# Hybrid decoder block on one core: the Strassen combinations of h (T1 to T4) made on GpSimd instead of VectorE

## Chip, cores and metric

The kernel runs on one NeuronCore of a Trainium2 chip. The metric is the device time of one execution in microseconds; lower is better. The engines are called TensorE (PE in the views; PEld is its weight load), VectorE (DVE), ScalarE (ACT), GpSimd (POOL) and SyncE (SP, which issues nearly all DMAs here).

## The reference

One decoder block with S = 2048 rows, D = 1024 features, fp32 in and out. Cut to what matters:

```python
mod = c @ W_ada + b_ada                         # shift, scale, gate for mixer and FFN
h = rms_norm(x, g_pre) * (1 + scale) + shift
p = h @ W_in                                    # one combined input projection
# split into attention q|k|v, mLSTM q|k|v|o, mLSTM i|f pre-gates, branch gates A|B
yA = sliding_window_attention(rope(q), rope(k), v, sinks)     # window 128, 8 q heads, 2 kv heads
yB = sigmoid(o) * norm(mlstm_chunkwise(silu(conv4(q)), silu(conv4(k)), v, i, f))
merged = sigmoid(gA) * (yA @ W_A) + sigmoid(gB) * (yB @ W_B)
x = x + gate * rms_norm(merged @ W_out)
x = x + gate2 * rms_norm(swiglu(modulate(rms_norm(x))))       # FFN with its own W's
```

What concerns the change is `h` and a part of `h @ W_in`.

## The kernel before

**fp32 by halves.** TensorE multiplies in a reduced fp32 form (`fp32r`). Each operand is split into a high part (a cast) and a low part (the residue), and a product is three matmuls: hi by hi, hi by lo, lo by hi. For weights `split` makes them: ScalarE casts `whi` (L259, L256 where heads are paired), VectorE subtracts for `wlo` (L260, L257). For h, ScalarE writes the cast (L518) and the full value (L520) from the transposed block in PSUM, and VectorE writes the residue (L521); in the first block GpSimd does L521.

**Blocks.** The rows go in four blocks of 512 (`TB`), numbered 0 to 3, and two blocks make a superblock. `hprep(b)` makes h of block b, transposed, feature tile by feature tile (`one(k)`, eight of them). The wide columns of W_in are multiplied for a superblock at a time by a Strassen-Winograd scheme with seven products; h is its 2 x 2 grid: feature half by row block. The scheme needs, besides h itself, four combinations T1 to T4, each a 128 x 4 x 512 tile. The even block leaves two of the full-precision h tiles in T1 and T4, the odd block two in T3 and T2; after each pair of feature tiles `one(k)`, `one(k + 4)` of an odd block four subtractions in place (L534 to L537) finish column k of all four:

```python
T1 = T3 - T1;  T3 = T2 - T3;  T2 = T2 - T1;  T4 = T4 - T2
```

That is 16 subtractions of 128 x 512 in block 1 and 16 in block 3, 32 in all. `hsums` later copies a finished T tile by DMA (L545, issued by SP) into the buffer of its low part, casts it (L551, ScalarE) and subtracts (L552, VectorE): first for T2 and T4, later for T1 and T3. `pair_parts` then uses them in the seven products.

**What runs around it.** While blocks 1 and 3 are prepared, TensorE multiplies the k, v, q, o and gate columns of the even block with plain three-matmul products (accumulators `acc`, weights `whi` and `wlo`); VectorE also makes rotary embeddings of q and k (L757 to L761, with L771/L772 and L797/L798 for the transposed copies), the moving convolution of gate columns (L810 to L813), and softplus and scans of the gates (L835 to L868, with the transposes mix_1070 and mix_1120 on TensorE). ScalarE moves accumulators out of PSUM (L827 and others). Then follows attention for the even block: loads by SP (L903 to L908), scores, mask (L933), maximum (L938), exponential (L946, ScalarE), normalisation (L950, GpSimd), transposes (L956, issued through L209), and the products with v. L428 is the accumulation of `c W_ada`.

**What sets the order.** The Python code writes these stages as generators (streams) that yield estimated delays; `tick` and `finish` interleave them by a running estimate of TensorE's time. The framework's compile-time scheduler (`schedule_with_timeline_sim=True`) then orders each engine's instructions again by its own model. On the chip each engine runs its list in order and waits at semaphores. `mm` and `transpose` all issue through one line each, L204 and L209, so TensorE's rows are told apart by tile.

Of the kernel before, what the change touches and what calls it, by code (L numbers as in the profile page):

```python
# [15 lines left out]
ALU = mybir.AluOpType  # L16
# [55 lines left out]
def decoder_block(ctx: ExitStack, tc: tile.TileContext, a: dict, out: bass.AP, dbg=None):  # L72
    nc = tc.nc
    V, A, G, T = nc.vector, nc.scalar, nc.gpsimd, nc.tensor
# [18 lines left out]
    def nm(s):  # L93
        uid[0] += 1
        return f"{s}{uid[0]}"
# [4 lines left out]
    def mix_tile():  # L100
        return ps_mix.tile([P, 512], F32, tag="mix", name=nm("mix"))
# [7 lines left out]
    def big(shape, dtype=F32):  # L109
        t = bpool.tile([P, 2048], dtype, tag="big", name=nm("big"))  # L110
        return t.rearrange("p (k c) -> p k c", k=shape[0])
# [4 lines left out]
    def load_x(src, big, i):  # L116
        xb = big([2, D])
        nc.sync.dma_start(xb, src[i * 256:(i + 1) * 256, :].rearrange("(t p) c -> p t c", p=P))
        return xb
# [86 lines left out]
    def transpose(o, i):  # L206
        now[0] += 110.0
        k = i.shape[0]
        T.transpose(o, i, ident[:k, :k])  # L209
# [260 lines left out]
    def rsqrt_of_sumsq(ss, n, eps=EPS):  # L470

        ms = small.tile([P, 4], F32, tag="ms", name=nm("ms"), bufs=4)
        V.tensor_scalar(ms[:, :n], ss, 1.0 / D, eps, op0=ALU.mult, op1=ALU.add)  # L473
        r = small.tile([P, 4], F32, tag="rs", name=nm("rs"), bufs=6)
        G.tensor_tensor(r[:, :n], ms[:, :n], nhalf[:, :n], op=ALU.pow)  # L475
        return r
# [3 lines left out]
    def hc_part(name, i):  # L480
        st = HC.setdefault(name, [None, None])
        if st[i] is None:
            st[i] = big([4, TB], F32R)
        return st[i]

    def hprep(b, first=False):

        odd = b % 2
        xs = []
        xbs = x_first if first else [load_x(x_d[b * TB:(b + 1) * TB, :], big, i) for i in range(2)]  # L490
        V_NAMES = ("T3", "T2") if odd else ("T1", "T4")
        for n in V_NAMES:
            HR[n] = big([4, TB])
        vs = [HR[n] for n in V_NAMES]
        for i in range(2):
            xb = xbs[i]
            ss = small.tile([P, 4], F32, tag="ss", name=nm("ss"), bufs=4)
            for t in range(2):
                for hf in range(2):
                    A.activation(vs[i][:, 2 * t + hf, :], xb[:, t, hf * 512:(hf + 1) * 512], AF.Square,  # L500
                                 accum_out=ss[:, 2 * hf + t:2 * hf + t + 1])
            V.tensor_tensor(ss[:, 0:2], ss[:, 0:2], ss[:, 2:4], op=ALU.add)
            r = rsqrt_of_sumsq(ss[:, 0:2], 2)
            for t in range(2):
                if first:
                    A.activation(xb[:, t, :], xb[:, t, :], AF.Copy, scale=r[:, t:t + 1])
                else:
                    V.tensor_scalar(xb[:, t, :], xb[:, t, :], r[:, t:t + 1], None, op0=ALU.mult)
                xs.append(xb[:, t, :])
        yield L_X  # L510

        def one(k):
            name = f"{k // 4 + 1}{odd + 1}"
            hi, lo = (hc_part(name, i)[:, k % 4, :] for i in range(2))
            ps = mix_tile()
            for t in range(NT):
                transpose(ps[:, t * P:(t + 1) * P], xs[t][:, k * P:(k + 1) * P])
            A.activation(hi, ps, AF.Identity, scale=s1[:, k:k + 1], bias=sh1[:, k:k + 1])  # L518
            v = vs[k // 4][:, k % 4, :]
            A.activation(v, ps, AF.Identity, scale=s1[:, k:k + 1], bias=sh1[:, k:k + 1])  # L520
            (G if first else V).tensor_tensor(lo, v, hi.bitcast(F32), op=ALU.subtract)  # L521

        if not odd:
            for k in range(KD):
                one(k)
                yield L_HT
            return
        for k in range(4):
            one(k)
            yield L_HT  # L530
            one(k + 4)
            yield L_HT
            t1, t2, t3, t4 = (HR[n][:, k, :] for n in ("T1", "T2", "T3", "T4"))
            V.tensor_tensor(t1, t3, t1, op=ALU.subtract)  # L534
            V.tensor_tensor(t3, t2, t3, op=ALU.subtract)
            V.tensor_tensor(t2, t2, t1, op=ALU.subtract)
            V.tensor_tensor(t4, t4, t2, op=ALU.subtract)  # L537
            yield L_HT

    def hsums(names):  # L540
# [170 lines left out]
    def c_tile(n):  # L711
        C[n] = kvp.tile([P, MH, MD + 1], F32, tag="cst", name=nm("cst"), bufs=3)
        return C[n]

    hp0 = hprep(0, first=True)
    next(hp0)
    tables = {}
# [18 lines left out]
    def superblock(sb):  # L736
# [474 lines left out]
        def outputs(b):  # L1211
# [41 lines left out]
            def before_out():  # L1253
                if b == 0:
                    finish(R["ada_m"])
                    R_ada.append(spawn(ada_stream([(4, "scale"), (3, "shift"), (5, "gate")], 9000.0)))
                if b == b1 and b + 1 < NBLK:
                    HC.clear()
                    hps[b + 1] = spawn(hprep(b + 1))
                    tables[sb + 1] = rope_tables(sb + 1)  # L1260
                R["gg"] = big([2, D])[:, 0, :]
                nc.sync.dma_start(R["gg"], gg_m_d)
                if b == b0:
                    end_attention(2 * NT)
                    load_y(b1, 0)
                    load_g(b1, 0)
# [11 lines left out]
        def start():  # L1278
            hps[b1] = spawn(hprep(b1), L_HP2)
# [590 lines left out]
```

## Time and profile before

| | |
|---|---|
| median of 3 runs | 2711.97 us (2708.91 to 2712.32) |
| profiled execution, its own time | 2716.59 us |
| span of the profiled execution | 2714.9 us |
| mean granted TensorE clock | 0.99 |
| busy TensorE / VectorE / ScalarE / GpSimd | 2639.2 / 1986.2 / 1299.8 / 148.2 us |
| DMA | 511.90 MB, mean 189 GB/s |

A row of a timeline has start and duration in microseconds, then engine, line, operation, output tile, input tiles, shapes and types, a count, and in brackets the idle time before it with what ended that. Instructions of one engine overlap at their ends, so the price of one in a row of equal ones is the distance of their starts, not the duration. Tiles are named without numbers in the views of the trace and with them in the order of instructions.

### The profile page before, as it was taken

The numbers are of one execution on the slowest core, as the hardware profiler recorded it, in microseconds if no ns is written. First come the engines' busy times: TensorE is split into PE (matmuls) and PEld (weight loads), VectorE is DVE, ScalarE is ACT, GpSimd is POOL, SyncE is SP. The second block draws the span as 40 slices with busy tenths as digits, with TensorE's granted clock in tenths as the row PEclk, the third lists the DMA queues.
The fourth block names the chain that finished last, engine by engine and source line by source line (L and its number), as shares of the span: only waits on it lengthen the run. The fifth ranks groups of instructions, "written<-read, shape, count | busy, mean of one in ns | idle before, by whom it ended". The sixth has DMA issues, their size and how long they took to land.

```text
span 2714.9 us, 35793 instructions
## 1 busy us (share of the span) xinstructions
PE 2639.2 (97%) x12310; PEld 2138.9 (79%) x12310; DVE 1986.2 (73%) x3906; ACT 1299.8 (48%) x2558; POOL 148.2 (5%) x189
## 2 busy tenths in 40 slices
PE   6989999999998999999999999999999999999998
PEld 4867788888885678888887888888877888888886
DVE  7968788778695778876687777776677676766456
ACT  5556544444755564444563443335554333333444
POOL 2010001100101000110000000000000000000000
PEclk8999999999998999999999999999999999999999
DMA  7654355897574544678765564436675232324566
GB/s 249 206 184 157 128 172 179 269 340 248 196 235 147 196 138 138 213 231 291 251 224 198 175 201 152 155 113 213 215 271 188 97 117 86 113 97 144 186 210 217
DMA packets 353639, 511.90 MB, mean 189 GB/s; under 512 B 25120, under 2 KB 213660, under 8 KB 348208
## 3 DMA queue, kind: packets, MB, share of 16 engines
q1 hardware_dynamic: 353456, 509.61, 56.9%
q8 instruction: 97, 1.59, 0.2%
q14 instruction: 86, 0.70, 0.1%
HBM read 357.12 MB, written 144.02 MB: 185 GB/s over the span
## 4 chain that ended last, share of the span: by engine, by line
PE 85%; DVE 7%; DMA 4%; ACT 2%; issue 1%; POOL 0%; SPq 0%; DVEq 0%; ACTq 0%; POOLq 0%
PE acc L204 61%; PE mix L204 22%; PE mix L209 2%; DVE hl L1357 1%; DVE tm L428 1%; DMA raw<-as_d 1%; ACT tm L946 1%; ACT hl L1356 1%; DMA raw<-in_w_in_dram 1%; DMA at_d<-tx 0%; DMA big<-in_x_dram 0%; DVE wlo L260 0%; DMA tx<-in_w_ada_dram 0%; DVE w L1667 0%; DMA at<-at_d 0%
## 5 line engine op out<-in xcount | busy, mean ns | idle before, releaser
L204 PE MATMUL acc<-big,hl 128*128 128x512 f32 x3936 | 940.8, 394 | 4.3 <-ACT tx L827 1.8
L204 PEld LDWEIGHTS acc<-big,hl 128*128 128x128 f32 x3936 | 733.3, 188 | 172.5 <-issue 13.8
L1356 ACT CAST hl<-raw 128x512 fp32r<-128x512 f32 x732 | 440.1, 621 | 493.4 <-PE acc L204 222.2
L1357 DVE TENSOR_TENSOR hl<-raw,hl 128x512 fp32r<-128x512 f32 x732 | 496.3, 694 | 194.8 <-ACT hl L1356 194.0
L204 PE MATMUL acc<-whi,big 128*128 128x512 f32 (+1 forms) x1280 | 379.3, 377 | 10.8 <-ACT big L518 8.4
L204 PEld LDWEIGHTS acc<-whi,big 128*128 128x128 f32 x1280 | 236.2, 192 | 52.4 <-ACT big L518 8.5
L204 PE MATMUL mix<-big,hl 128*128 128x512 f32 x1056 | 263.9, 391 | 1.7 <-ACT hl L1356 1.1
L204 PE MATMUL acc<-wlo,big 128*128 128x512 f32 (+1 forms) x640 | 241.2, 379 | 6.4 <-DVE wlo L260 6.4
L204 PE MATMUL acc<-hl,hl 128*128 128x512 f32 x1008 | 237.4, 393 | 5.1 <-DVE hl L1357 3.4
L204 PEld LDWEIGHTS mix<-big,hl 128*128 128x128 f32 x1056 | 197.9, 188 | 45.9 <-ACT hl L1356 1.9
L204 PEld LDWEIGHTS acc<-hl,hl 128*128 128x128 f32 x1008 | 187.0, 188 | 50.9 <-DVE hl L1357 8.8
L204 PE MATMUL mix<-hl,hl 128*128 128x512 f32 x792 | 182.7, 391 | 1.3 <-DVE hl L1357 0.9
L204 PEld LDWEIGHTS mix<-hl,hl 128*128 128x128 f32 x792 | 147.9, 188 | 35.3 <-DVE hl L1357 3.1
L204 PE MATMUL acc<-big,whi 128*128 128x512 f32 x512 | 157.4, 393 | 0.0
L260 DVE TENSOR_TENSOR wlo<-raw,whi 128x1024 fp32r<-128x1024 f32 (+1 forms) x96 | 109.0, 1137 | 65.5 <-ACT whi L259 59.8
L259 ACT CAST whi<-raw 128x1024 fp32r<-128x1024 f32 (+1 forms) x96 | 94.3, 983 | 123.8 <-PE acc L204 110.4
L204 PEld LDWEIGHTS acc<-wlo,big 128*128 128x128 f32 x640 | 123.7, 193 | 28.3 <-DVE wlo L260 8.6
L475 POOL TENSOR_TENSOR rs<-ms,nhalf 128x1 f32<-128x1 f32 (+1 forms) x56 | 42.6, 772 | 1617.5 <-DVE ms L473 1610.5
L204 PE MATMUL mix<-hcT4h,hl 128*128 128x512 f32 x352 | 117.7, 395 | 0.7 <-ACT hl L1356 0.7
L204 PE MATMUL acc<-hcT2h,hl 128*128 128x512 f32 x352 | 117.6, 394 | 0.0
L204 PEld LDWEIGHTS acc<-big,whi 128*128 128x128 f32 x512 | 95.4, 188 | 19.2
L204 PE MATMUL acc<-big,wlo 128*128 128x512 f32 x256 | 97.7, 393 | 0.0
(330 smaller groups left out, 3491.5 us busy)
## 6 DMA issues: line engine op xcount, KB each, us to landing
raw<-in_w_in_dram SPq DMA_DIRECT2D x48, 1024.0 KB
as_d<-w SPq DMA_DIRECT2D x154, 256.0 KB
raw<-as_d SPq DMA_DIRECT2D x70, 512.0 KB
raw<-in_w_ffn_gate_dram SPq DMA_DIRECT2D x22, 1024.0 KB
raw<-in_w_ffn_up_dram SPq DMA_DIRECT2D x22, 1024.0 KB
raw<-ws_d SPq DMA_DIRECT2D x40, 512.0 KB
y_d<-tm SPq DMA_DIRECT2D x64, 256.0 KB
tx<-in_w_ada_dram SPq DMA_DIRECT2D x64, 256.0 KB
```

The source lines that it names most:

```text
L204: T.matmul(o, lhsT=lhsT, rhs=rhs, start=start, stop=stop, skip_group_check=resumed)
L209: T.transpose(o, i, ident[:k, :k])
L259: A.copy(hv, src)
L260: V.tensor_tensor(lv, src, hv.bitcast(F32), op=ALU.subtract)
L428: V.scalar_tensor_tensor(acc, raw[:, k, :], c_, acc, op0=ALU.mult, op1=ALU.add)
L475: G.tensor_tensor(r[:, :n], ms[:, :n], nhalf[:, :n], op=ALU.pow)
L946: A.activation(sc[g][:, j, :], sc[g][:, j, :], AF.Exp, bias=nm_[:, hd:hd + 1], accum_out=sums[:, hd:hd + 1])
L1356: A.copy(v(hi), src)
L1357: V.tensor_tensor(v(lo), src, v(hi).bitcast(F32), op=ALU.subtract)
```

## The change

The four subtractions that finish a column of T1 to T4 are issued on GpSimd (`G`) instead of VectorE (`V`). Nothing else in the code is different.

```diff
             t1, t2, t3, t4 = (HR[n][:, k, :] for n in ("T1", "T2", "T3", "T4"))
-            V.tensor_tensor(t1, t3, t1, op=ALU.subtract)
-            V.tensor_tensor(t3, t2, t3, op=ALU.subtract)
-            V.tensor_tensor(t2, t2, t1, op=ALU.subtract)
-            V.tensor_tensor(t4, t4, t2, op=ALU.subtract)
+            G.tensor_tensor(t1, t3, t1, op=ALU.subtract)
+            G.tensor_tensor(t3, t2, t3, op=ALU.subtract)
+            G.tensor_tensor(t2, t2, t1, op=ALU.subtract)
+            G.tensor_tensor(t4, t4, t2, op=ALU.subtract)
             yield L_HT
```

The scheduler orders the other instructions anew in two stretches, in superblock 0 from about 75 us on and in superblock 1 from about 735 us on. GpSimd's list gains the 16 subtractions of each odd block, in one piece.

VectorE, block 1, just ahead of the weight residue wlo_999, before (big_204, big_538, big_539 and big_205 are T1, T3, T2 and T4; tx_9xx are row tiles of k, v and gate columns):

```order
L537 TENSOR_TENSOR big_205<-big_205,big_539 128x512 [waits DVE_49]
L521 TENSOR_TENSOR big_666<-big_538,big_665 128x512 [waits Activation_49]
L534 TENSOR_TENSOR big_204<-big_538,big_204 128x512
L757 TENSOR_TENSOR tx_966<-tx_964,sin_478 128x2x32 [waits DMAHW0_49,Activation_49]
L758 TENSOR_TENSOR tx_966<-tx_964,sin_478 128x2x32
L759 TENSOR_TENSOR tx_924<-tx_924,cos_479 128x128 [waits DVE_49]
L812 TENSOR_TENSOR gt<-tx_964,b_if 128x4
L811 COPY v_last<-tx_924 128x128 [waits DVE_49]
L813 TENSOR_TENSOR gt<-tx_964,b_if 128x4
L537 TENSOR_TENSOR big_205<-big_205,big_539 128x512 [waits DVE_49]
L260 TENSOR_TENSOR wlo_999<-raw_618,whi_998 128x1024 [waits PE_49,Activation_49]
```

The same place now:

```order
L757 TENSOR_TENSOR tx_966<-tx_964,sin_478 128x2x32 [waits DMAHW0_49,Activation_49]
L758 TENSOR_TENSOR tx_966<-tx_964,sin_478 128x2x32
L810 TENSOR_TENSOR tx_964<-tx_964,v_last 128x128 [waits DMAHW7_49,DVE_49]
L812 TENSOR_TENSOR gt<-tx_964,b_if 128x4
L813 TENSOR_TENSOR gt<-tx_964,b_if 128x4
L759 TENSOR_TENSOR tx_964<-tx_964,cos_479 128x128 [waits DVE_49]
L811 COPY v_last<-tx_964 128x128 [waits DVE_49]
L760 TENSOR_TENSOR tx_964<-tx_964,tx_966 128x2x32 [waits DVE_49]
L521 TENSOR_TENSOR big_690<-big_539,big_689 128x512 [waits Activation_49]
L761 TENSOR_TENSOR tx_964<-tx_964,tx_966 128x2x32
L260 TENSOR_TENSOR wlo_999<-raw_618,whi_998 128x1024 [waits PE_49,Activation_49]
```

The subtractions are gone from the rows ahead of wlo_999, and work of later row tiles and of the last feature tile (big_690) has moved up into their place.

TensorE, the start of the first attention (mix_1120 are the transposes of the gates' scans, mix_1142 and mix_1143 the first scores, acc_1541 to acc_1544 a later projection), before:

```order
L204 MATMUL acc_1541<-whi_1657,big_689 128x264
L204 MATMUL acc_1542<-whi_1657,big_689 128x264
L204 MATMUL acc_1543<-whi_1657,big_689 128x264
L204 MATMUL acc_1544<-whi_1657,big_689 128x264
L209 MATMUL mix_1120<-ident,tm_1084 128x68 x4
L204 MATMUL mix_1142<-at_1042 128x128
```

Now:

```order
L204 MATMUL acc_1032<-whi_1278,big_421 128x512
L204 MATMUL acc_1032<-wlo_1279,big_421 128x512
L204 MATMUL acc_1032<-whi_1278,big_422 128x512
L204 MATMUL acc_1541<-whi_1426,big_665 128x264
L209 MATMUL mix_1120<-ident,tm_1084 128x68 x4
L204 MATMUL mix_1142<-at_1042 128x128
```

The transposes and the scores now come right after the first matmul of that projection instead of far into it, some 75 rows earlier.

TensorE, a later group of the same attention (mix_1466 and mix_1467 are scores, mix_1522 and mix_1552 the transposes of normalised scores, mix_1567 the product with v), before:

```order
L204 MATMUL mix_1466<-at_1359 128x256
L204 MATMUL mix_1467<-at_1359 128x256
L209 MATMUL mix_1522<-ident,tm_1368 128x128 x4
L209 MATMUL mix_1552<-ident,tm_1369 128x128 x4
L204 MATMUL mix_1567<-tm_1527,at_1328 64x512
```

Now, where between the scores mix_1467 and these rows stand 32 rows of a projection, of which the last are shown:

```order
L204 MATMUL acc_1789<-whi_1874,big_689 128x512
L204 MATMUL acc_1789<-wlo_1875,big_689 128x512
L209 MATMUL mix_1522<-ident,tm_1368 128x128 x4
L204 MATMUL acc_1789<-whi_1874,big_690 128x512
L204 MATMUL acc_1790<-whi_1874,big_689 128x512
L204 MATMUL acc_1790<-wlo_1875,big_689 128x512
L209 MATMUL mix_1552<-ident,tm_1369 128x128 x4
```

Projection matmuls now stand between the scores of this group and its transposes, and between the transposes themselves.

Two further places: on SP, L545 for T2 and T4 now waits for GpSimd where it waited for VectorE, with the attention loads L906 and L908 behind it; on ScalarE, the casts L551 of T2 (big_1608) now stand ahead of the cast L259 of whi_1426, before behind it.

## Prediction

> **What bounds the kernel now.** I read the page's engine line first, then its chain of waits, then the windows around the two places where L534 to L537 run, and there the timelines of VectorE, GpSimd and TensorE. The page gives:
>
> ```profile
> PE 2639.2 (97%) x12310; PEld 2138.9 (79%) x12310; DVE 1986.2 (73%) x3906; ACT 1299.8 (48%) x2558; POOL 148.2 (5%) x189
> PE 85%; DVE 7%; DMA 4%; ACT 2%; issue 1%; POOL 0%; SPq 0%; DVEq 0%; ACTq 0%; POOLq 0%
> ```
>
> TensorE is busy for 97% of the span: all its waits together are 2714.9 - 2639.2 = 75.7 us, so VectorE work costs time only where TensorE stands waiting for it. The windows say where that can be; after the window stand its length, then busy PE, PEld, DVE, ACT, POOL, granted clock, DMA share and GB/s.
>
> ```profile
> 75.00:105.00 30.00, 28.45 (x165) 24.41 (x164) 29.80 (x80) 19.20 (x31) 0.00 (x0) 1.00 0.66 201
> 105.00:125.00 20.00, 17.95 (x127) 16.83 (x126) 16.61 (x41) 10.91 (x24) 0.00 (x0) 0.91 0.95 316
> 125.00:190.00 65.00, 58.15 (x291) 39.41 (x290) 42.00 (x136) 38.38 (x120) 9.38 (x9) 0.95 0.49 149
> 740.00:772.00 32.00, 29.82 (x198) 26.92 (x197) 29.09 (x79) 19.16 (x33) 0.00 (x0) 1.00 0.56 178
> 772.00:800.00 28.00, 24.71 (x148) 21.34 (x147) 23.04 (x59) 12.62 (x26) 0.00 (x0) 0.95 0.90 313
> ```
>
> The 32 subtractions run at 75 to 105 us (block 1) and 736 to 776 us (block 3). There VectorE is the engine without room (29.80 of 30 us, 29.09 of 32) and GpSimd does nothing. The page's 73% hides this. TensorE still loses little there, 1.55 us of the first 30, since VectorE is just in time. How nearly just in time is read from three rows (start, duration, engine):
>
> ```profile
> 74.05 0.68 DVE L521 TENSOR_TENSOR big<-big,big 128x512 fp32r<-128x512 f32 x1
> ...
> 91.05 1.22 DVE L260 TENSOR_TENSOR wlo<-raw,whi 128x1024 fp32r<-128x1024 f32 x1
> ...
> 92.78 0.39 PE L204 MATMUL acc<-wlo,big 128*128 128x512 f32 x1
> ```
>
> From 74.05 to the end of this weight residue (wlo_999 in the order) at 92.27 VectorE works without a gap, and TensorE uses the residue at 92.78: 0.51 us of slack. What lengthens VectorE's queue here stops TensorE.
>
> **What goes off VectorE.** Two neighbouring subtractions give the price by their starts:
>
> ```profile
> 93.59 0.68 DVE L534 TENSOR_TENSOR big<-big,big 128x512 f32<-128x512 f32 x1
> 94.19 0.68 DVE L535 TENSOR_TENSOR big<-big,big 128x512 f32<-128x512 f32 x1
> ```
>
> 0.60 us each, so 16 x 0.60 = 9.6 us of VectorE per odd block. Nine of the 16 lie ahead of wlo_999 (three L534, two of each other line): -5.4 us.
>
> **What moves up.** The scheduler fills the room: by the order of VectorE, three L521, two L759, six L760 or L761, two L810 and two L811 now stand ahead of wlo_999. Their prices, again by starts:
>
> ```profile
> 102.66 0.22 DVE L761 TENSOR_TENSOR tx<-tx,tx 128x64 f32<-128x64 f32 x1
> 102.79 0.29 DVE L810 TENSOR_TENSOR tx<-tx,v_last 128x128 f32<-128x128 f32 x1
> 102.99 0.17 DVE L837 TENSOR_SCALAR sp<-sp 128x16 f32<-128x16 f32 x1
> ```
>
> L761 takes 0.13, L810 0.20; with L760 and L811 like the first, L759 like the second, and L521 at 0.60, it is 1.8 + 4 x 0.20 + 8 x 0.13 = +3.7 us.
>
> **What GpSimd costs VectorE.** The trace has no GpSimd L534, but L521 is the same kind, two 128x512 SBUF operands, and the first block runs it on GpSimd. One pair runs beside VectorE's L428 and one while VectorE is elsewhere; L950 beside L257 and beside a VectorE operation that reads PSUM (mix) complete the picture:
>
> ```profile
> 26.19 0.88 DVE L428 SCALAR_TENSOR_TENSOR tm<-big,c_sb,tm 128x256 f32<-128x256 f32 x2
> 27.03 2.81 POOL L521 TENSOR_TENSOR big<-big,big 128x512 fp32r<-128x512 f32 x2 [8.98 <-ACT big L520]
> 27.18 2.94 DVE L428 SCALAR_TENSOR_TENSOR tm<-big,c_sb,tm 128x256 f32<-128x256 f32 x2
> 55.12 2.63 POOL L521 TENSOR_TENSOR big<-big,big 128x512 fp32r<-128x512 f32 x2 [8.00 <-ACT big L520]
> ...
> 132.05 1.28 DVE L257 TENSOR_TENSOR wlo<-raw,whi 128x512 fp32r<-128x512 f32 x2
> 139.11 2.14 DVE L257 TENSOR_TENSOR wlo<-raw,whi 128x512 fp32r<-128x512 f32 x2
> 139.35 1.35 POOL L950 TENSOR_TENSOR tm<-tm,sums 128x512 f32<-128x512 f32 x1 [0.40 <-DVE sums L949]
> ...
> 177.93 1.04 POOL L950 TENSOR_TENSOR tm<-tm,sums 128x512 f32<-128x512 f32 x1 [0.40 <-ACT tm L972]
> 177.96 0.69 DVE L973 TENSOR_TENSOR tm<-mix,tm 128x512 fp32r<-128x512 f32 x1 [0.16 <-ACT tm L972]
> ```
>
> Alone, one GpSimd operation takes 2.63 / 2 = 1.31 us. The same two L428 take 0.88 alone and 2.94 beside two GpSimd operations: 2.06 lost, 1.03 for each. L257 loses 0.86 to one L950. L973, with an operand in PSUM, keeps its 0.69 us. So a GpSimd subtraction takes from VectorE, where both operands are in SBUF, more than the 0.60 it relieves it of. The bounds are 0 (as L973) and 1.31 (the whole operation); I take 1.03, the row with the same GpSimd instruction.
>
> [...]
>
> **First place.** GpSimd needs some 1.8 us per operation when it alternates with VectorE, and its input rows come in time: by 105 us about 15 of the 16 have run. Ahead of wlo_999: -5.4 + 3.7 + 15 x 1.03 = +13.8, less 1 for the four L772, which read PSUM like L973, less the slack of 0.5: TensorE is 12.2 us late. Then it gains back waits:
>
> ```profile
> 117.70 0.59 PE L204 MATMUL acc<-wlo,big 128*128 128x264 f32 x1 [2.05 <-DVE wlo L260]
> ...
> 167.22 1.70 PE L204 MATMUL mix<-at 64*128 64x256 f32 x24 [2.75 <-DMA at<-at_d]
> 170.71 1.39 PE L209 MATMUL mix<-ident,tm 128*128 128x128 f32 x8 [1.79 <-DVE tm L933]
> 177.59 0.65 PE L209 MATMUL mix<-ident,tm 128*128 128x128 f32 x4 [1.42 <-POOL tm L950]
> 179.03 1.04 PE L209 MATMUL mix<-ident,tm 128*128 128x128 f32 x4 [0.79 <-POOL tm L950]
> ```
>
> The 2.05 goes, since everything else had 12 us more. The four attention waits are 6.75 together; in the new order of TensorE the attention starts some 75 rows earlier and projection matmuls stand between its steps, so I count 5.5 of them as covered. Net +12.2 - 2.05 - 5.5 = +4.7 us. If the cover fails, it is +10.
>
> **Second place.** Between the next two VectorE rows twelve of the 16 go:
>
> ```profile
> 736.24 0.68 DVE L534 TENSOR_TENSOR big<-big,big 128x512 f32<-128x512 f32 x1
> 741.82 0.69 DVE L521 TENSOR_TENSOR big<-big,big 128x512 fp32r<-128x512 f32 x1 [2.40 <-DMA x1n<-tm]
> ...
> 770.62 0.69 DVE L536 TENSOR_TENSOR big<-big,big 128x512 f32<-128x512 f32 x1
> 772.30 1.22 DVE L260 TENSOR_TENSOR wlo<-raw,whi 128x1024 fp32r<-128x1024 f32 x1
> ...
> 773.57 0.50 PE L204 MATMUL acc<-wlo,big 128*128 128x512 f32 x1 [0.69 <-DVE wlo L260]
> ...
> 790.68 0.39 PE L204 MATMUL acc<-whi,big 128*128 128x264 f32 x1 [1.42 <-ACT tx L827]
> ```
>
> -12 x 0.60 + 16 x 1.03 = +9.3; four L772 lie beside GpSimd (-2), and the gap of 2.40 at 741.82 takes 2 of it: +5.3 at the residue of 772.30, which already has TensorE waiting 0.69, so there is no slack. The 1.42 at 790.68 is given back: +3.9.
>
> **Sum:** +4.7 + 3.9 = +8.6 us. The profiled execution (2716.59 us, span 2714.9) would become 2725.2; against the median of 2711.97 it is 2720.6, which I put down as 2721. By the price p per GpSimd operation the sum is 31p - 23.3 or so, which is zero at p = 0.75, 3 at 0.86 and 17 at 1.31.
>
> **What is hidden.** The subtractions are needed only by the second half of the block's work, through L545's copy and L551's cast:
>
> ```profile
> 90.82 0.83 ACT L520 ACTIVATE big<-mix,sh,s 128x512 f32<-128x512 f32 x1
> 105.26 1.22 SPq L545 DMA_DIRECT2D big<-big  x2
> 108.78 0.63 ACT L259 CAST whi<-raw 128x528 fp32r<-128x528 f32 x1 [0.30 <-PE acc L204]
> 111.09 1.14 ACT L551 CAST big<-big 128x512 fp32r<-128x512 f32 x2 [1.19 <-DMA big<-big]
> ```
>
> L545 now waits for GpSimd, and on ScalarE the casts of L551 now stand ahead of L259, whose result starts the next projection. From L545's issue to the first cast are 5.83 us, four casts take 2.3 and L259 0.63: GpSimd's end plus 8.7. Its last inputs are the ScalarE row at 90.82 and the last L521, just ahead of wlo_999, so it ends about 106, and L259 about 115, while TensorE, 12 late, asks for it at 109.3 + 12 = 121. The late TensorE is the cover. Behind L545 on SP stand the attention loads L906 and L908 and weight loads; behind the subtractions on GpSimd stand L858, a memset that the gates' L861 needs, and L950, which are wanted later still.
>
> **Rivals.**
> 1. [...] Chance 0.14.
> 2. It cancels: p near 0.75, since the two engines find gaps (VectorE's own semaphore waits, PSUM operands) better than in the three samples. 2710 to 2717. Chance 0.22.
> 3. [...] Chance 0.12.
> 4. GpSimd becomes the bound: its chain ends after 112.6 us where TensorE is on time, or after 121 - 8.7 where it is late, and L545, L906 and L551 with it. If each operation takes 2.2 us instead of 1.8, or the L521 it waits for comes late, it ends 5 to 6 later; TensorE stops for what exceeds the cover, 5 in each place on top of 8.6: 2731. Chance 0.10.
>
> All 32 rows do change engine, so that nothing happens is no case.
>
> **How the numbers follow.** The forecast, 2721, has 0.42 (its own range 2716 to 2726). A measurement can tell about 0.2%, 5.4 us. Faster by more: rival 1, 0.14. Within: rival 2 and the low edge of the forecast, 0.24. Slower by more: 0.62. The range runs from 2705 (half of rival 1 left out) to 2734 (beyond rivals 3 and 4).
>
> **What would show it.** Right: GpSimd at 1.3 to 1.8 us per subtraction; VectorE's L521 and L260 stretched from 0.6 to above 1 us beside it; a new TensorE wait of about 12 us in all ahead of the wlo_999 matmuls near 92 us, fewer waits in the attention. Wrong: VectorE rows unstretched; or TensorE waiting near 115 us for ScalarE's L259 (rival 4); or the attention waits unchanged.

## The result, and the profile after

The changed kernel takes 2720.16 us (median of 7 runs, 2719.25 to 2723.11) against 2711.97 us (7 runs, 2708.91 to 2715.5). The ratio is 1.0034 with an interval of 1.0024 to 1.0044, so it is slower by 9.2 us (6.5 to 11.9; 8.2 between the two medians). The forecast was 2721.

The two profiled executions of the kernel before (2716.59 and, in a later run, 2717.67) lie some 5 us above its median, while that of the changed kernel (2720.58, span 2718.9) lies on its own; the difference of two spans, 4.0 us, is therefore too small, and totals below go by the medians of the runs. Inside a profile I use an anchor: one GpSimd row that has the same 11.5 us of waiting before it in every kernel, near 500 us, behind the first place and ahead of the second.

The page of the changed kernel, engine line and chain of waits:

```profile
PE 2637.5 (97%) x12310; PEld 2139.1 (79%) x12310; DVE 1993.5 (73%) x3874; ACT 1300.0 (48%) x2558; POOL 206.3 (8%) x221
PE 88%; DVE 5%; DMA 3%; ACT 2%; issue 1%; POOL 0%; SPq 0%; DVEq 0%; POOLq 0%; ACTq 0%
```

VectorE executes 32 instructions fewer and is busy 7.3 us longer (1986.2 before). That is the result in one line: what left it came back as stretched rows. TensorE is busy as long as before, within 1.7 us; by the page alone nothing happened. The windows at the first place show where it happened (length, then busy PE, PEld, DVE, ACT, POOL, clock, DMA share, GB/s):

```profile
75.00:105.00 30.00, 19.41 (x112) 16.31 (x111) 30.00 (x50) 14.47 (x26) 28.10 (x16) 0.85 0.47 143
105.00:125.00 20.00, 20.00 (x108) 16.76 (x107) 16.78 (x43) 12.93 (x24) 1.23 (x2) 0.96 0.98 324
125.00:190.00 65.00, 62.95 (x336) 43.81 (x334) 39.88 (x135) 37.10 (x117) 8.84 (x9) 1.00 0.51 150
```

In 75 to 105 us VectorE is full as before, but 50 instructions are counted in it instead of 80; TensorE is idle for 10.59 us of the 30 instead of 1.55. In 125 to 190 us it then has fewer gaps (62.95 busy against 58.15). The anchor gives the net of the first place, first before, then after:

```profile
501.11 1.02 POOL L1078 TENSOR_TENSOR cf<-vr,nhalf 128x4 f32<-128x4 f32 x1 [11.47 <-DVE vr L1076]
```

```profile
507.02 1.02 POOL L1078 TENSOR_TENSOR cf<-vr,nhalf 128x4 f32<-128x4 f32 x1 [11.46 <-DVE vr L1076]
```

Everything behind the first place is 5.9 us later. The changed kernel's timeline of GpSimd, first and last of the 16 subtractions of block 1:

```profile
72.42 9.39 POOL L534 TENSOR_TENSOR big<-big,big 128x512 f32<-128x512 f32 x2 [5.85 <-ACT big L520]
81.77 3.50 POOL L535 TENSOR_TENSOR big<-big,big 128x512 f32<-128x512 f32 x2
...
87.92 1.27 POOL L536 TENSOR_TENSOR big<-big,big 128x512 f32<-128x512 f32 x1
...
104.49 1.28 POOL L537 TENSOR_TENSOR big<-big,big 128x512 f32<-128x512 f32 x1
```

And VectorE's in the same time:

```profile
76.42 0.68 DVE L521 TENSOR_TENSOR big<-big,big 128x512 fp32r<-128x512 f32 x1
78.86 0.68 DVE L772 SCALAR_TENSOR_TENSOR tx<-mix,tx 128x512 fp32r<-128x512 f32 x1
79.46 1.18 DVE L521 TENSOR_TENSOR big<-big,big 128x512 fp32r<-128x512 f32 x1
80.57 1.88 DVE L772 SCALAR_TENSOR_TENSOR tx<-mix,tx 128x512 fp32r<-128x512 f32 x3
84.06 1.30 DVE L757 TENSOR_TENSOR tx<-tx,sin 128x64 f32<-128x64 f32 x1
...
100.87 1.28 DVE L761 TENSOR_TENSOR tx<-tx,tx 128x64 f32<-128x64 f32 x1
102.07 1.21 DVE L260 TENSOR_TENSOR wlo<-raw,whi 128x1024 fp32r<-128x1024 f32 x1
```

The reader should see two things: a short row such as L761, 0.13 us before, can wait out nearly a whole GpSimd subtraction (1.28 here, by starts 1.20), while L772, whose operand mix lies in PSUM, keeps its pitch of about 0.6. The residue wlo_999 (last row) is ready at 103.28 instead of 92.27. TensorE's timeline shows who waited:

```profile
92.63 0.31 PE L209 MATMUL mix<-ident,tx 128*128 128x128 f32 x1 [4.29 <-DVE tx L761]
95.53 0.45 PE L209 MATMUL mix<-ident,tx 128*128 128x128 f32 x1 [2.59 <-DVE tx L761]
...
102.29 0.30 PE L209 MATMUL mix<-ident,tx 128*128 128x128 f32 x1 [2.51 <-DVE tx L761]
...
102.90 0.93 PE L204 MATMUL acc<-whi,big 128*128 128x512 f32 x2
103.63 0.63 PE L204 MATMUL acc<-wlo,big 128*128 128x512 f32 x1
104.05 1.05 PE L204 MATMUL acc<-whi,big 128*128 128x512 f32 x2
104.91 0.63 PE L204 MATMUL acc<-wlo,big 128*128 128x512 f32 x1
...
106.54 0.39 PE L204 MATMUL acc<-whi,big 128*128 128x512 f32 x1
106.77 0.40 PE L204 MATMUL acc<-wlo,big 128*128 128x512 f32 x1
```

They are three waits, 9.39 us together, not on wlo_999 but on L761: transposes of k rows that the new order puts ahead of it. The residue is first used at 104.91 (before 92.78) without a wait of its own. And the matmuls behind the waits are slower: from 103.63 to 104.91 three starts take 1.28 us, 0.43 each, from 106.54 to 106.77 one takes 0.23.

### The profile page after: what moved, and what is told of

It is laid out like the page before. It is cut to its first block, busy times and chain, and to the rows that moved or that the text cites. A ratio compares the mean times of both kernels' runs of the same rounds, so it can differ in the third digit from the quotient of the medians.

```text
span 2718.9 us, 35799 instructions
## 1 busy us (share of the span) xinstructions
PE 2637.5 (97%) x12310; PEld 2139.1 (79%) x12310; DVE 1993.5 (73%) x3874; ACT 1300.0 (48%) x2558; POOL 206.3 (8%) x221
## 4 chain that ended last, share of the span: by engine, by line
PE 88%; DVE 5%; DMA 3%; ACT 2%; issue 1%; POOL 0%; SPq 0%; DVEq 0%; POOLq 0%; ACTq 0%
PE acc L204 63%; PE mix L204 23%; PE mix L209 2%; DVE hl L1357 1%; DMA raw<-in_w_ffn_down_dram 1%; DVE tm L428 1%; ACT hl L1356 1%; DMA raw<-as_d 1%; ACT tm L946 1%; DMA at<-at_d 0%; DMA big<-in_w_ada_dram 0%; DVE big L1357 0%; DVE w L1667 0%; DMA raw<-in_w_ffn_gate_dram 0%; DMA big<-in_x_dram 0%
## 5 line engine op out<-in xcount | busy, mean ns | idle before, releaser
L260 DVE TENSOR_TENSOR wlo<-raw,whi 128x1024 fp32r<-128x1024 f32 (+1 forms) x96 | 110.3, 1150 | 68.7 <-ACT whi L259 62.9
L259 ACT CAST whi<-raw 128x1024 fp32r<-128x1024 f32 (+1 forms) x96 | 94.5, 984 | 123.4 <-PE acc L204 113.6
```

What stands on the lines that cost most here:

```text
L259: A.copy(hv, src)
L260: V.tensor_tensor(lv, src, hv.bitcast(F32), op=ALU.subtract)
```

## The experiments

Ratios are against the kernel before, run on the same chip alongside.

**The kernel before once more**, unchanged.

> The kernel before, run once more for a second profile. The median should be 2712 within 3 us. Open is where the first profiled execution (2716.59 us) was 4.6 us above the median: theory one, in the second place (736 to 980 us), so that the 3.3 us which the changed kernel seems to gain there are chance; then L950 of the second attention stands 3 to 5 us earlier than in the first profile. Theory two, elsewhere or evenly; then the GpSimd rows up to 980 us stand within 1 us of the first profile, and the gain of the changed kernel in the second place is real.

2713.88 us, ratio 1.0002 (0.9993 to 1.0012). Its anchor lies 0.45 us earlier than in the first profile, so shifts of this anchor by some 2 us and more mean something. Neither theory fits whole: the rows of L950 near 930 us stand within 0.3 us of the first profile, those near 980 us 1.3 earlier, so that in the second place differences below 2 us say nothing.

**One block at a time.**

```diff
+            E = G if b == 1 else V
-            G.tensor_tensor(t1, t3, t1, op=ALU.subtract)
+            E.tensor_tensor(t1, t3, t1, op=ALU.subtract)
...
```

> Only block 1 has the subtractions on GpSimd, block 3 keeps them on VectorE; the order of block 1 is that of the changed kernel. If the places add, the pair of profiles says +5.9 us (GpSimd rows at 443 to 640 us are that much later): 2718. The sum of the prediction said +4.7: 2717. If the whole loss of 8 us is made in block 1: 2720.

> Only block 3 has them on GpSimd. The prediction's sum said +3.9 us: 2716. The pair of profiles says -3.3: 2709. If the profile of before was long by chance just there, it is in between, 2712 to 2714.

Block 1 alone: 2718.05 us, 1.0021 (1.0012 to 1.0030), +5.7 us; its anchor is 5.6 late. Block 3 alone (`b == 3`): 2713.34 us, 1.0005 (0.9996 to 1.0013), +1.4 us (-1 to +3.5). So the first place costs what the anchor says, and the second little or nothing that can be told from zero: neither the +3.9 of the sum nor the -3.3 of the pair of profiles, but what was expected if the first profile was long there by chance. It does stall; two of its waits, by TensorE's timeline of the kernel with block 3 alone:

```profile
747.09 0.39 PE L204 MATMUL acc<-wlo,big 128*128 128x264 f32 x1 [2.25 <-DVE wlo L260]
...
778.77 0.45 PE L209 MATMUL mix<-ident,tx 128*128 128x128 f32 x1 [5.89 <-DVE tx L762]
```

In the changed kernel all waits between 740 and 870 us are 18.35 us together, 14.84 before; those between 870 and 960 are 2.09, before 5.1. What the second place loses in one stretch, 3.5 us, the next returns, 3.0. The second profile of the kernel before has 16.96 and 3.85 there, and against that it is 1.4 lost and 1.8 returned.

**GpSimd writes but does not read.** The subtractions are left out, and GpSimd writes a constant, an operation without SBUF input. VectorE's order stays. The memsets wait for no input, so eight of block 1's sixteen run before 63 us; the other eight run between 74 and 91.

```diff
-            G.tensor_tensor(t1, t3, t1, op=ALU.subtract)
...
+            for t in (t1, t3, t2, t4):
+                G.memset(t, 0.0)
```

> Leaves the 32 subtractions out; GpSimd writes a constant into the same tiles instead, in the same places, without reading. The order is that of the changed kernel nearly everywhere. Theory of blocked reads: VectorE's operations with two SBUF operands run at their own length beside it, the TensorE waits for L761 in 90 to 103 us go, and the attention keeps its cover: some 8 us faster than before, 2703 to 2706. Rival, the new order is what costs: about 2720 as the changed kernel. Second rival, GpSimd blocks VectorE whatever it does: between the two, 2712 or more.

2698.58 us, 0.9949 (0.9936 to 0.9961): 14 us faster than before and 22 faster than the changed kernel, faster than even the first theory had it, with the same work taken off VectorE and, from the L521 at 79.46 to the residue, the same instructions in the same order on it. Its VectorE rows, and one memset:

```profile
79.47 0.67 DVE L521 TENSOR_TENSOR big<-big,big 128x512 fp32r<-128x512 f32 x1
...
85.10 0.53 POOL L535 MEMSET big<- 128x512 f32 x1 [4.37 <-DVE big L521]
85.22 0.22 DVE L755 TENSOR_TENSOR tx<-tx,sin 128x64 f32<-128x64 f32 x1
...
89.85 1.23 DVE L260 TENSOR_TENSOR wlo<-raw,whi 128x1024 fp32r<-128x1024 f32 x1
90.99 0.22 DVE L755 TENSOR_TENSOR tx<-tx,sin 128x64 f32<-128x64 f32 x1
```

L755 here is L757 of the changed kernel: 0.22 us beside a memset, 1.30 beside a subtraction. Five memsets fall into this stretch of VectorE, and no row beside them is longer than elsewhere. The same stretch of VectorE, from the start of this L521 to the end of wlo_999, takes 90.99 - 79.47 = 11.52 us here and 103.20 - 79.46 = 23.74 in the changed kernel. The difference of 12.2 (12.7 without some 0.5 of idle time in this one) falls to 14 GpSimd subtractions: 0.87 to 0.91 us each. That is the disputed price, on the kernel itself, with the GpSimd operations that ran beside L772 counted in. It isn't spread evenly: of the 37 instructions in this stretch of the changed kernel's VectorE 13 are stretched, the short ones by 1.1 us, and the others keep their time. In 75 to 105 us TensorE is busy 28.79 us, and from 125 to 190 it is idle for only 0.79:

```profile
75.00:105.00 30.00, 28.79 (x169) 24.73 (x167) 27.09 (x81) 21.51 (x37) 4.24 (x9) 1.00 0.88 271
...
125.00:190.00 65.00, 64.21 (x305) 43.75 (x304) 42.45 (x125) 34.41 (x98) 7.28 (x7) 1.00 0.57 174
```

**GpSimd reads one operand instead of two.**

```diff
-            G.tensor_tensor(t1, t3, t1, op=ALU.subtract)
+            G.tensor_copy(t1, t3)
...
```

> Leaves the 32 subtractions out; GpSimd copies one tile into another in their places, so it reads one operand and writes. VectorE's order in block 1 is that of the changed kernel row by row. Theory, a read of GpSimd is enough to block VectorE's operations with two SBUF operands: each copy costs nearly its own length, 1.0 to 1.3 us, and the time is 2716 to 2722. Rival, it takes two operands on both sides: about 2699, as with the written constant.

2702.08 us, 0.9958 (0.9942 to 0.9973). The expectation took the copy to be as long as the subtraction. It is not:

```profile
72.20 7.54 POOL L534 COPY big<-big 128x512 f32<-128x512 f32 x2 [5.86 <-ACT big L520]
...
83.43 0.63 DVE L757 TENSOR_TENSOR tx<-tx,sin 128x64 f32<-128x64 f32 x1
...
84.49 0.61 POOL L534 COPY big<-big 128x512 f32<-128x512 f32 x1
...
92.46 1.63 DVE L260 TENSOR_TENSOR wlo<-raw,whi 128x1024 fp32r<-128x1024 f32 x1
94.01 0.63 DVE L757 TENSOR_TENSOR tx<-tx,sin 128x64 f32<-128x64 f32 x1
```

One copy takes about 0.6 us, and L757 beside it 0.63: between 0.22 and 1.30. So reading one operand is enough to block, and a short VectorE row that is stretched lasts about as long as the GpSimd operation beside it (L757 here 0.63 beside copies of 0.61; L758 of the changed kernel, at 85.28, 1.33 beside an L536 of 1.29). Over the same stretch of VectorE (79.23 to 94.01 us, 14.78 against 11.52) that is 3.3 us for 13 copies, about 0.25 each. VectorE's rows show this, not the time, whose interval overlaps that of the kernel with memsets.

In the profiled execution (2706.38 us, the slowest of five) the anchor stands at 500.94: the first place gains nothing, where the memsets gain 7.6 (493.53). Behind it TensorE ran at half clock for 13.7 us (the window is shown further down), worth at most half of that, 6.9 us, by estimate. Whether the other four executions had this too isn't known.

**Half of them.** T1 and T3 on VectorE, T2 and T4 on GpSimd.

```diff
-            V.tensor_tensor(t2, t2, t1, op=ALU.subtract)
-            V.tensor_tensor(t4, t4, t2, op=ALU.subtract)
+            G.tensor_tensor(t2, t2, t1, op=ALU.subtract)
+            G.tensor_tensor(t4, t4, t2, op=ALU.subtract)
```

> T1 and T3 on VectorE, T2 and T4 on GpSimd: half of the dose. If the loss goes with the number of GpSimd operations, half of the 9 us: 2716. If each GpSimd operation costs 0.9 us of VectorE against the 0.6 it saves and nothing else happens, 16 x 0.3 = +5 where TensorE waits: 2712 to 2717. If the new order (attention earlier) comes in already with half the relief, below 2712.

2712.12 us, 0.9999 (0.9989 to 1.0009). Half the dose does not make half the loss of 9.2; it makes none that can be measured, at the low edge of the second theory.

**The subtractions on VectorE, but later.** The room on VectorE was worth 14 us when nothing blocked it. These kernels look for that room without GpSimd.

```diff
+    last_wlo = [None]
...
-            V.tensor_tensor(lv, src, hv.bitcast(F32), op=ALU.subtract)
+            last_wlo[0] = V.tensor_tensor(lv, src, hv.bitcast(F32), op=ALU.subtract)
...
-            V.tensor_tensor(t1, t3, t1, op=ALU.subtract)
...
+        if "T4" in names:
+            for k in range(4):
+                t1, t2, t3, t4 = (HR[n][:, k, :] for n in ("T1", "T2", "T3", "T4"))
+                with tc.issue_after(last_wlo[0].ins):
+                    V.tensor_tensor(t1, t3, t1, op=ALU.subtract)
...
+                yield L_HT
```

> All 32 subtractions on VectorE, but queued behind the weight residues of the even block, where the attention starts: VectorE's rows ahead of the wlo_999 matmuls are free of them as in the changed kernel, the attention starts at the same early row of TensorE, and GpSimd stays empty. Theory: what the changed order is worth is had without the blocking, so near the kernel with the written constant: 2698 to 2704. Rival: the 9.6 us of VectorE per odd block have to be paid anyway, now in the attention: 2708 to 2713.

> All on VectorE, as four subtractions of 128 x 2048 at the end of an odd block's preparation instead of sixteen of 128 x 512. It saves VectorE 12 x 0.07 = 0.8 us per odd block and moves half of the work behind wlo_999; TensorE's order keeps the late attention. Expected 2709 to 2713; if the room ahead of wlo_999 alone were what the constant-writing kernel gained, 2700.

The first, above: 2717.77 us, 1.0018 (1.0009 to 1.0026). The second, where each of the four differences is one 128x2048 instruction at the end of the block's preparation: 2717.27 us, 1.0015 (1.0006 to 1.0025). Both missed. The 0.07 us per joined instruction is 2 x 0.60 - 1.13 in the profile before, where the L260 of 128x1024 at 85.11 is followed by the next row at 86.24. In the second TensorE waits for VectorE's work on the gates (2.72 us at 120.16), as it did not before; whether that is all of its loss is open. In the first, thirteen of the 16 come out between 110 and 124 us, ahead of a later residue:

```profile
124.77 0.59 PE L204 MATMUL acc<-wlo,big 128*128 128x264 f32 x1 [4.77 <-DVE wlo L262]
```

So the same kernel with `yield 6000.0` at the head of the `if`, which spreads the columns between steps of the attention, and one with 12000.0:

> As the kernel with the subtractions deferred on VectorE (2717.77), but hsums gives them out column by column 6000 units of the program's clock later, between the steps of the first attention: one column ahead of the residue wlo_1607, one behind it, two behind wlo_1639. If that kernel lost only because its sixteen stood ahead of wlo_1619 (TensorE waited 4.77 us there), 2708 to 2713. If VectorE's 9.6 us cost wherever they stand, 2715 to 2719.

> The same with 12000 units: all sixteen stand behind the last residue of the even block, where VectorE has most room. If the place is what counts, the gain of the early attention shows: 2700 to 2708, faster than both. If the time of VectorE has to be paid anyway, 2712 to 2718.

The first takes 2703.9 us, 0.9973 (0.9962 to 0.9983), faster than the kernel before, than the changed one, and than either theory had it; the second 2706.98, 0.9983 (0.9972 to 0.9994), inside the range of its first theory but not faster than the first. In the first the residues keep their place among the subtractions; VectorE's timeline, one TensorE row, and the window after them:

```profile
110.25 0.69 DVE L262 TENSOR_TENSOR wlo<-raw,whi 128x528 fp32r<-128x528 f32 x1
110.87 0.67 DVE L544 TENSOR_TENSOR big<-big,big 128x512 f32<-128x512 f32 x1
...
122.58 0.69 DVE L262 TENSOR_TENSOR wlo<-raw,whi 128x528 fp32r<-128x528 f32 x1
```

```profile
127.71 0.39 PE L204 MATMUL acc<-wlo,big 128*128 128x264 f32 x1 [0.57 <-DVE wlo L262]
```

```profile
125.00:190.00 65.00, 61.61 (x313) 43.65 (x311) 54.29 (x144) 40.75 (x113) 9.55 (x9) 1.00 0.63 203
```

The wait at the residue is 0.57 instead of 4.77, and VectorE is now busy 54.29 of these 65 us (42.00 before): the work went to where it had room. TensorE's idle time there is 3.39 us, 6.85 before.

**The other GpSimd work beside VectorE.** L521 of the first block on VectorE instead of GpSimd; then this together with the last kernel.

```diff
-            (G if first else V).tensor_tensor(lo, v, hi.bitcast(F32), op=ALU.subtract)
+            V.tensor_tensor(lo, v, hi.bitcast(F32), op=ALU.subtract)
```

> The subtractions stay on VectorE as before; instead the eight L521 of the first block, which before leaves to GpSimd, go to VectorE too, so that nothing on GpSimd reads while VectorE is full. Four of the eight stood beside L428 and cost it 1.03 us each in the first profile; on VectorE they take 0.60: -1.7 us, and the other four fall into VectorE's idle time: 2709 to 2711. Rival: VectorE is on the path to the first matmuls and pays 4.8 us more: 2713 to 2717.

> Both edits together: the subtractions deferred column by column on VectorE, and the eight L521 of the first block on VectorE. They touch different stretches (before 63 us; from 75 us on), so if they add: 0.9973 x 0.9991 of the time before, 2701.5. If the first edit's gain was only another alignment of loads in later stretches, which the new start shifts again: 2704 to 2710.

Alone 2708.71 us, 0.9991 (0.9982 to 0.9999); together 2707.72, 0.9987 (0.9976 to 0.9997). The two do not add: the time is what the second theory said. By the anchor the first place keeps both gains (501.11 before, 494.17 and 499.00 alone, 490.33 together). They are lost behind it. From the anchor to the first row of the same kind behind 1000 us the kernel before takes 608.75 us (607.38 in its second profile), the two edits alone 600.27 and 601.22, both together 608.54. The edit of the first block changes nothing in that stretch but the order of some instructions and the start, so these alone seem able to move it by some 7 us (one profile each); how is open.

## Why the prediction was right, and where only its sum was

**The mechanism** held. A GpSimd subtraction took more from VectorE than the 0.60 us it relieved it of; with memsets in place of the subtractions the kernel is 14 us faster than before, with the subtractions 9.2 slower. Rival 1, p up to 0.5 us and VectorE on time, had the right price for that other case (2698.58 measured, 2702 given) and not for the change. The runs show what made the difference: a 128x64 row of VectorE took 0.22 us beside a memset (L755), which reads nothing, 0.63 beside a copy, which reads one operand, and 1.30 beside a subtraction, which reads two (L757).

**The price p** was mis-sized: 1.03 taken, 0.87 to 0.91 measured. The sample pair of L428 overstated it, the one L257 row (0.86) did not. Rival 3, the whole 1.31, falls. At 0.87 the formula gives 31 x 0.87 - 23.3 = +3.7 us: same, not slower. That 2721 came out is therefore partly luck: over both places the price was 5 us too high (31 x 0.16), the cover below 2.4 too generous, and of the 9.2 measured the two places account for 7.1.

**The give-back in the attention** was mis-sized: 5.5 of 6.75 us counted as covered, 6.75 - 2.05 - 1.65 = 3.05 were. By TensorE's timeline of the changed kernel the waits of 165 to 190 us are gone, but new ones stand earlier, 2.05 together, and 1.65 more come from 190 us on:

```profile
134.63 0.66 PE L209 MATMUL mix<-ident,tm 128*128 128x128 f32 x4 [1.75 <-POOL tm L950]
...
136.07 0.65 PE L209 MATMUL mix<-ident,tm 128*128 128x128 f32 x4 [0.30 <-POOL tm L950]
```

The 2.05 at the residue near 117 us did vanish, as said.

**Slow matmuls** were missing as a term. From 102.90 to 106.54 nine matmuls take 3.64 us, where nine at 0.23 take 2.1: +1.6, of which 0.9 ahead of 104.91. The granted clock, in finer windows of the changed kernel:

```profile
92.60:95.00 2.40, 0.31 (x1) 0.14 (x1) 2.40 (x8) 0.27 (x1) 1.01 (x1) 0.54 0.04 12
95.00:99.00 4.00, 3.48 (x9) 2.83 (x10) 4.00 (x12) 0.27 (x1) 3.88 (x2) 0.50 0.26 75
99.00:102.00 3.00, 0.78 (x2) 0.09 (x1) 3.00 (x3) 0.00 (x0) 3.00 (x3) 0.90 0.00 0
```

It is 0.54 and 0.50 after the wait of 4.29 us. The slow matmuls behind 102.29, at 0.53 from 102.90 to 106.54, follow a wait of only 2.51 us, in a stretch of some 3 us (99 to 102) with 0.78 of work. The kernel with copies goes further: a clock of 0.50 follows a window in which TensorE was busy for 2.70 of 3.40 us, with one wait of 0.70, and lasts 13.7 us. So no long wait is needed for it, and what sets its start and its end these runs do not show:

```profile
111.10:114.50 3.40, 2.70 (x28) 2.45 (x28) 3.09 (x8) 3.40 (x8) 0.00 (x0) 1.00 1.06 412
114.50:128.20 13.70, 13.70 (x65) 12.66 (x64) 10.59 (x32) 9.65 (x32) 0.61 (x1) 0.50 0.37 125
```

The kernel before has slow matmuls as well, behind its wait of 2.05, and they go with that wait:

```profile
117.70:121.10 3.40, 3.40 (x15) 3.40 (x16) 3.34 (x8) 0.00 (x0) 0.00 (x0) 0.50 0.99 360
```

From 118.08 to 120.94 thirteen matmuls take 2.86 us there, where 0.12 each, as a little later, is 1.6: -1.3. So the missing term is +1.6 and -1.3, near nothing in sum.

**First place:** 4.7 forecast; the runs show 5.7 (block 1 alone), the anchor 5.9. What GpSimd takes from VectorE ahead of wlo_999 stood in the sum as 15 x 1.03 - 1 = 14.4 and is 12.2 to 12.7. The 1.8 us for a GpSimd operation beside VectorE has its like in one pair of the profile before, 3.58 / 2 = 1.79 beside L428:

```profile
43.54 3.58 POOL L521 TENSOR_TENSOR big<-big,big 128x512 fp32r<-128x512 f32 x2 [13.71 <-ACT big L520]
```

In the changed kernel the first two subtractions take 9.35 us (72.42 to 81.77) and the other 14 take 24.0 (81.77 to 105.77), 1.71 each. TensorE's lateness at wlo_999 is all the same as forecast, 12.1 (92.78 to 104.91) against 12.2, and that is luck: TensorE stops at three k transposes, which the order of instructions would have shown, and 2.6 us of its matmuls, 0.9 of that from half clock, stand between the last of them and the residue. From there on, with the 0.7 of slow matmuls behind 104.91, the -2.05 and -1.3 at 117.70 and the cover of 3.05, the timelines give 12.1 + 0.7 - 3.35 - 3.05 = 6.4, half a microsecond above the anchor.

**Second place:** 3.9 forecast, 1.4 (-1 to +3.5) measured. At 0.87 the term is 16 x 0.16 = 2.5 smaller, which is 1.4; the losses to 870 us and the return behind it, which the prediction did not look at, nearly cancel as well. Which of the two readings holds is not settled. The two places alone make 7.1 us, the change 9.2 (6.5 to 11.9): within the intervals.

**Hidden work** stayed hidden, rival 4 did not come, but with less room than the 6 us forecast. GpSimd's last subtraction ends at 105.77 (106 forecast). But SP issues L545 only at 110.89, behind six transfers of L801, which the forecast's chain had left out; then come ScalarE, and TensorE's first need of whi_1426 in the second matmul of the last row, about 121.7:

```profile
110.89 1.20 SPq L545 DMA_DIRECT2D big<-big  x2
115.51 2.19 ACT L551 CAST big<-big 128x512 fp32r<-128x512 f32 x4 [4.12 <-DMA big<-big]
117.60 0.63 ACT L259 CAST whi<-raw 128x528 fp32r<-128x528 f32 x1
```

```profile
121.49 0.51 PE L204 MATMUL acc<-whi,big 128*128 128x512 f32 x2
```

L259 ends at 118.2, so 3.5 us of cover were left.

Of the forecast's signs, GpSimd at 1.3 to 1.8 us for most subtractions, stretched VectorE rows and fewer attention waits came; the wait ahead of wlo_999 came as three, elsewhere. Rival 2, that it cancels, was nearer than its chance of 0.22 looks: by p alone it would have been it.

## What to carry to other kernels

Where VectorE is full of operations with two SBUF operands, price a move to GpSimd by what its operations take from VectorE, here two thirds of the length of each (0.87 to 0.91 of 1.31 us), and not by what VectorE is spared (0.60). A VectorE row of 0.13 us can wait out nearly a whole one (1.20 for L761). Before moving work to another engine, look for a later time on the same one: the same subtractions, spread between the steps of the attention, are worth 7.4 us here (2703.9 against 2711.3). That gain isn't secure, since with one more edit elsewhere only 3.5 us were left of it (0.9987). And when TensorE is made to wait, read the granted clock of the matmuls behind the wait (0.50 here behind 4.29 us), in the kernel before as well (0.50 behind 2.05).

## What was not expected of the hardware

- GpSimd was held off while VectorE issued operations with two SBUF inputs one behind the other: two L534 took 9.39 us, where two such operations alone (L521 at 55.12, before) take 2.63, and two copies 7.54. VectorE's rows up to 78.86 are not stretched (L521 takes 0.68 and L760 0.42, as before); there it turns to L772, with its operand in PSUM, and between that and 81.77 both L534 fit. That this is what let them in is inferred, not tried.
- A GpSimd copy or memset of 128x512 is less than half as long as a subtraction (0.61 and 0.53 against 1.31 us), and a copy, though it blocks, takes only 0.25 us or so from VectorE.
